# A pad of 32 bytes ahead of the ring of split weights

## The chip, the core and the metric

The kernel runs on one core of one Trainium2 chip. The metric is the device time of one execution in microseconds. One program is built and launched once; all inputs lie in the chip's memory when the clock starts.

## What is computed

One layer of a hybrid decoder trunk on a sequence of 256 tokens of width 4096, in float32. Cut to what matters:

```
h    = rmsnorm(x, ln_g)                       # 256 x 4096
proj = h @ w_in                               # 4096 x 12288: pool, attention, state space and their gates
y_pool = pool_mixer(p_x, w_pool, pool_scale)
y_attn = stick_breaking_attention(q, k, v)    # 16 heads of 128
y_ssm  = s5_mixer(s_u, ...)                   # scan over the tokens, GELU, then a GLU: h @ w_glu (1024 x 2048)
y      = concat(rmsnorm(branch) * silu(gate)) # 256 x 4096
x      = x + y @ w_out                        # 4096 x 4096
out    = rmsnorm(x, final_g)
```

The three products with w_in, w_glu and w_out are nearly all of the arithmetic. The result has to be of float32 quality.

## The kernel before, in words

**Precision by splitting.** Every big product is made of three fp32r matmuls (one pass of TensorE each, with operands rounded by the engine). Each operand is split into a rounded part, hi, and the rest, lo; the product is x_hi w_hi + x_hi w_lo + x_lo w_hi. ScalarE makes hi by a copy that rounds (line 126), VectorE makes lo as the difference (line 236).

**Which operand is which.** The activations are stationary: the tile `xhl` holds 32 slices of 128 rows, each as hi and lo for 256 tokens (128 partitions x 64 KiB). The weights are moving: they arrive in pieces of 128 x 1024 floats (tile `w`, four buffers), are split into a pair of tiles `hi` and `lo` of 4 KiB per partition each, and stream through TensorE in runs of 512 columns (2 KiB per partition) into a PSUM bank. So every matmul in the main loops loads 128 x 128 floats as the stationary operand and moves 128 x 512. Line 376 is x_hi w_hi, line 383 is x_hi w_lo, line 384 is x_lo w_hi:

```
o = ps[t][:, at:at + wide]
made = T.matmul(o, stat[:, slot, 0, sl], hi[:, n], start=begin, stop=False, skip_group_check=True)
T.matmul(o, stat[:, slot, 0, sl], lo[:, n], start=False, stop=False, skip_group_check=True)
made = T.matmul(o, stat[:, slot, 1, sl], hi[:, n], start=False, stop=end, skip_group_check=True)
```

**The ring.** The pairs are kept in a ring of four (`RING`), in the pool named `stream`, and splitting runs two pieces ahead of the products (`SPLIT_AHEAD`). In the output projection two more pairs are added from another pool (tiles `hix`, `lox`).

**Stages.** First come 24 units of 16 pieces for w_in, four units of 4 pieces for w_glu (whose stationary operand is the tile `hhl`), then four units of 32 pieces for w_out. Between the units' matmuls the program places the side work: the scan's small matmuls (line 714, 742), transposes against an identity (lines 434 and 846), pooling (515, 516, 523), attention (775 to 806). In the output projection a part of the pieces goes through `mm_seven` (line 315), which makes seven products where the plain form makes eight, with sums of rows `y` as stationary operand in some of them. Side work for VectorE and ScalarE is handed out by counters per piece; SyncE issues nearly all loads. The order on each engine is made by the scheduler when the program is built.

**Where tiles lie.** A partition's memory is a stack from the left and one from the right. Every tile takes a multiple of 32 bytes. From the left come the constants and small sums (pool `const`), then `xhl`, then the ring, then everything that opens later on the left (masks, u, attention's tiles, `hhl`, the rows `y`, the two added pairs). The loads `w`, the working tiles of 4 KiB and the scan's tiles lie on the right. The pools are opened in this order:

```
cp = pool("const")
xp = pool("xhl")
wp = pool("stream")
bp = pool("base", side="right")
fp = pool("loads", side="right")
```

In the built program `xhl` begins at byte 5792 of each partition, the four `hi` at 71328, 75424, 79520 and 83616, the four `lo` at 87712, 91808, 95904 and 100000. All of these are 32 above a multiple of 64. The same holds for the other tiles that the fp32r matmuls read (`hhl`, `y`, the added pairs, attention's `tneg`, `ah`, `ax`), for the pooling's and attention's operands and for the mask in bf16; of the matmuls' operands only the identity (byte 4224) is at a multiple of 64. The runs of 512 columns and the slices of 128 columns are whole multiples of 64 bytes, so each operand begins where its tile does, up to such a multiple.

Of the kernel before, what the change touches and what calls it, by code (L numbers as in the profile page):

```python
# [12 lines left out]
F32 = mybir.dt.float32  # L13
# [7 lines left out]
P = 128  # L21
# [62 lines left out]
def body(tc, a, out, ctx):  # L84
# [13 lines left out]
    def pool(name, bufs=1, **kw):  # L98
        return ctx.enter_context(tc.tile_pool(name=name, bufs=bufs, **kw))

    cp = pool("const")
    xp = pool("xhl")
    wp = pool("stream")
    bp = pool("base", side="right")
    fp = pool("loads", side="right")
# [1154 lines left out]
def build(nc, arrays):  # L1260
    a = {k: nc.dram_tensor("in_" + k, v.shape, mybir.dt.from_np(v.dtype), kind="ExternalInput").ap() for k, v in arrays.items()}
    out = nc.dram_tensor("out", (L, D), F32, kind="ExternalOutput").ap()
    with tile.TileContext(nc, schedule_with_timeline_sim=True) as tc:
        with ExitStack() as ctx:
            body(tc, a, out, ctx)
# [8 lines left out]
```

## Time and profile before

| what | value |
|---|---|
| median of 2 runs | 1505.53 us (1505.07 to 1505.99) |
| the profiled execution's own time | 1505.46 us |
| its span, first to last instruction | 1503.7 us |
| mean granted TensorE clock | 0.997 |
| TensorE matmul busy | 1491.0 us, 6850 matmuls |
| weight load busy | 1231.9 us |
| VectorE busy | 1224.2 us |
| ScalarE busy | 883.6 us |
| data moved | 424.50 MB, mean 282 GB/s |

How to read it: PE is TensorE's matmuls, PEld its loads of the stationary operand, which run beside the matmuls. A matmul's duration in the profile is longer than the distance to the next one's start, since matmuls are pipelined: in the main loops a matmul of 0.39 us starts every 0.23 us. A busy share of 99% therefore says that TensorE is never out of work, not how fast it works. The distance between the starts, called the pitch here, is what adds up to the span.

### The profile page before, as it was taken

The page shows a single profiled execution, that of the slowest core. Times are in us where ns is not written, and L with a number is a line of the kernel's source. Part 1 is how long each engine was busy: PE and PEld are TensorE (multiplying, and loading weights), DVE is VectorE, ACT ScalarE, POOL GpSimd, SP SyncE. Part 2 cuts the span into 40 slices and gives each one's busy share as a digit, 9 for nine tenths or more (in the row PEclk, how much of TensorE's full clock was granted, in tenths as well). Part 3 has the DMA queues.
Part 4 walks back from the last instruction along what each step waited for, and adds up shares of the span by engine and source line. Part 5 has one row for each costly group of instructions (what it writes and reads, how often), then busy time and mean ns, then how long its engine had stood idle before and what let it go on. Part 6 is the DMA issues. An engine that isn't in the chain of part 4 may idle for free.

```text
span 1503.7 us, 19837 instructions
## 1 busy us (share of the span) xinstructions
PE 1491.0 (99%) x6850; PEld 1231.9 (82%) x6850; DVE 1224.2 (81%) x1876; ACT 883.6 (59%) x1166; POOL 15.2 (1%) x31
## 2 busy tenths in 40 slices
PE   9999999999999999999999999999999999999996
PEld 7888888888888888888888888888888888888885
DVE  7479978898999898998975555686657998989887
ACT  7655456665655555555655544665546776757574
POOL 0000000000000000000000000000000000000000
PEclk9999999999999999999999999999999999999998
DMA  9866556676788887888788788798977998989795
GB/s 357 308 226 207 194 172 212 197 229 232 267 301 306 295 302 249 307 298 300 239 293 284 272 299 282 268 338 314 339 246 249 367 369 324 333 307 353 271 365 222
DMA packets 129364, 424.50 MB, mean 282 GB/s; under 512 B 15472, under 2 KB 21360, under 8 KB 129264
## 3 DMA queue, kind: packets, MB, share of 16 engines
q1 hardware_dynamic: 115504, 398.17, 75.3%
q10 hardware_dynamic: 10000, 10.92, 2.5%
q0 software_dynamic: 3760, 14.16, 2.5%
q8 instruction: 53, 0.87, 0.2%
q14 instruction: 47, 0.39, 0.1%
HBM read 371.28 MB, written 48.76 MB: 279 GB/s over the span
## 4 chain that ended last, share of the span: by engine, by line
PE 99%; DVE 1%; ACT 0%; issue 0%; DVEq 0%
PE pm L376 27%; PE pm L383 27%; PE pm L384 27%; PE p L315 8%; PE pm L315 6%; PE ps_c L846 1%; PE ps_bu L714 1%; PE ps_y L742 1%; PE ps_t L434 0%; PE ps_z L775 0%; PE ps_p L523 0%; PE ps_i L151 0%; PE ps_z L793 0%; PE ps_av L805 0%; PE ps_av L806 0%; PE ps_av L804 0%
## 5 line engine op out<-in xcount | busy, mean ns | idle before, releaser
L236 DVE TENSOR_TENSOR lo<-w,hi 128x1024 fp32r<-128x1024 f32 (+1 forms) x531 | 619.0, 1172 | 226.2 <-ACT hi L126 224.2
L126 ACT ACTIVATE hi<-w 128x1024 fp32r<-128x1024 f32 (+1 forms) x531 | 537.7, 1019 | 441.0 <-PE pm L384 357.9
L383 PE MATMUL pm<-lo,xhl 128*128 128x512 f32 x1710 | 667.1, 390 | 0.0
L384 PE MATMUL pm<-hi,xhl 128*128 128x512 f32 x1710 | 666.8, 390 | 0.0
L376 PE MATMUL pm<-hi,xhl 128*128 128x512 f32 x1710 | 658.2, 391 | 0.0
L376 PEld LDWEIGHTS pm<-hi,xhl 128*128 128x128 f32 x1710 | 321.2, 188 | 66.0 <-ACT hi L126 0.6
L383 PEld LDWEIGHTS pm<-lo,xhl 128*128 128x128 f32 x1710 | 321.2, 188 | 65.8 <-DVE lo L236 0.7
L384 PEld LDWEIGHTS pm<-hi,xhl 128*128 128x128 f32 x1710 | 321.2, 188 | 65.5
L236 DVE TENSOR_TENSOR lo<-t,hi 128x1024 fp32r<-128x1024 f32 x84 | 100.5, 1219 | 10.7 <-ACT hi L126 10.0
L126 ACT ACTIVATE hi<-t 128x1024 fp32r<-128x1024 f32 x84 | 87.3, 1055 | 34.0 <-PE pm L384 11.6
L315 PE MATMUL pm<-hi,xhl 128*128 128x512 f32 x168 | 65.3, 390 | 0.0
L315 PE MATMUL p<-hi,xhl 128*128 128x512 f32 x168 | 65.2, 389 | 0.0
L315 PE MATMUL p<-hi,y 128*128 128x512 f32 x168 | 64.5, 389 | 0.0
L126 ACT ACTIVATE tr<-et,pw 128x32 f32<-128x32 f32 (+3 forms) x128 | 45.2, 385 | 22.4 <-DVE et L123 9.1
L123 DVE SCALAR_TENSOR_TENSOR et<-et,pw,tr 128x16 f32<-128x16 f32 (+3 forms) x256 | 55.7, 274 | 2.9 <-ACT tr L126 2.7
L114 DVE TENSOR_TENSOR pre<-pre 128x512 f32<-128x512 f32 (+2 forms) x72 | 49.6, 689 | 1.0
L729 DVE TENSOR_TENSOR_SCAN tb<-rho,ta 128x256 f32<-128x256 f32 x64 | 40.5, 674 | 0.2
L315 PEld LDWEIGHTS p<-hi,xhl 128*128 128x128 f32 x168 | 31.5, 188 | 6.5
L315 PEld LDWEIGHTS p<-hi,y 128*128 128x128 f32 x168 | 31.5, 188 | 6.5
L315 PEld LDWEIGHTS pm<-hi,xhl 128*128 128x128 f32 x168 | 31.5, 188 | 6.5
L315 PE MATMUL p<-lo,y 128*128 128x512 f32 x84 | 32.7, 389 | 0.0
L315 PE MATMUL p<-lo,xhl 128*128 128x512 f32 x84 | 32.7, 389 | 0.0
(278 smaller groups left out, 1171.9 us busy)
## 6 DMA issues: line engine op xcount, KB each, us to landing
w<-in_ws SPq DMA_DIRECT2D x492, 512.0 KB, 5.0
pre<-in_ws SPq DMA_DIRECT2D x68, 512.0 KB, 7.1
sums<-pre SPq DMA_DIRECT2D x68, 512.0 KB, 5.6
t<-sums SPq DMA_DIRECT2D x68, 512.0 KB, 7.3
w<-in_ws SPq DMA_DIRECT2D x38, 256.0 KB, 7.0
xsq<-in_xr SPq DMA_DIRECT2D x8, 512.0 KB, 6.7
o<-in_xr SPq DMA_DIRECT2D x8, 512.0 KB, 7.7
xt<-in_xT SPq DMA_DIRECT2D x15, 256.0 KB, 6.1
```

Source lines behind the costliest of these rows:

```text
L114: V.tensor_tensor(o, x, y, op)
L123: V.scalar_tensor_tensor(o, x, s, y, op0, op1)
L126: return S.activation(o, x, f, **kw)
L236: low = V.tensor_tensor(dst_lo, src, dst_hi.bitcast(F32), ALU.subtract)
L315: T.matmul(o, stat[:, p, :], pair[q][:, n], start=start and k == 0, stop=stop and k == 2, skip_group_check=True)
L376: made = T.matmul(o, stat[:, slot, 0, sl], hi[:, n], start=begin, stop=False, skip_group_check=True)
L383: T.matmul(o, stat[:, slot, 0, sl], lo[:, n], start=False, stop=False, skip_group_check=True)
L384: made = T.matmul(o, stat[:, slot, 1, sl], hi[:, n], start=False, stop=end, skip_group_check=True)
L714: T.matmul(ps[:, c, :], b3r[:, j, c, :], u3r[:, j, :], start=c == 0, stop=True, skip_group_check=True)
L729: V.tensor_tensor_scan(tb[:, c, :], rho[:, pr:pr + 1].broadcast_to([P, L]), ta[:, c, :], 0.0, ALU.mult, ALU.add)
L742: made = T.matmul(ps[32 * j:32 * j + 32, 0:L], cf[:, j, c, :], ss[j][:, c, :], start=c == 1, stop=c == 0, skip_group_check=True)
L846: T.transpose(ps[:, (c * 2 + t) * P:(c * 2 + t + 1) * P], z[:, t, (h * 2 + c) * P:(h * 2 + c + 1) * P], ident)
```

## The change

A pool of its own with one tile of 32 bytes per partition is opened between `xhl` and the ring. Nothing writes or reads the tile.

```
 
     cp = pool("const")
     xp = pool("xhl")
+    pool("even").tile([P, 8], F32, name="even")
     wp = pool("stream")
     bp = pool("base", side="right")
     fp = pool("loads", side="right")
```

In the built program `xhl` stays at 5792; the `hi` begin at 71360, 75456, 79552 and 83648, the `lo` at 87744, 91840, 95936 and 100032, which are multiples of 64. All that stands behind them on the left moves by 32 as well, and so also begins at multiples of 64: the moving operands of the main loops and of attention's fp32r matmuls, and with them `hhl` and the rows `y`, the stationary operands of the GLU and of a part of the output projection. The tiles on the right stay where they were. The instructions, their order on every engine and their waits are the same as before.

More of the change, by code (lines that the diff above doesn't have):

```diff
@@ L102, in body @@
     xp = pool("xhl")
+    pool("even").tile([P, 8], F32, name="even")
     wp = pool("stream")
```

## The prediction

> **What bounds the kernel now.** I read the profile page first: the totals of the engines, the granted clock, and the shares of the chain that ended last.
>
> ```profile
> span 1503.7 us, 19837 instructions
> PE 1491.0 (99%) x6850; PEld 1231.9 (82%) x6850; DVE 1224.2 (81%) x1876; ACT 883.6 (59%) x1166; POOL 15.2 (1%) x31
> PEclk9999999999999999999999999999999999999998
> DMA  9866556676788887888788788798977998989795
> PE 99%; DVE 1%; ACT 0%; issue 0%; DVEq 0%
> L126 ACT ACTIVATE hi<-w 128x1024 fp32r<-128x1024 f32 (+1 forms) x531 | 537.7, 1019 | 441.0 <-PE pm L384 357.9
> ```
>
> TensorE is the chain from end to end, at the full granted clock, and does not wait for its operands: it is ScalarE that stands idle, 357.9 us of it until line 384's matmul gives a ring buffer back. The time is thus a count of matmuls times their pitch. Four views, each limited to one line over the whole span, count those of the main loops (lines 376, 383, 384 and 315 in this order; the number behind the x):
>
> ```profile
> 0.00:1503.70 1503.70, 684.06 (x1778) 334.01 (x1778) 1.00 0.81 282
> 0.00:1503.70 1503.70, 693.19 (x1778) 334.02 (x1778) 1.00 0.81 282
> 0.00:1503.70 1503.70, 693.03 (x1778) 333.94 (x1778) 1.00 0.81 282
> 0.00:1503.70 1503.70, 201.35 (x882) 165.39 (x882) 1.00 0.81 282
> ```
>
> That is 6216, of which the last 12 are 256 columns wide: 6204 matmuls of 512 columns. Their pitch I take from the timeline of the last stage, whose first column is the start:
>
> ```profile
> 1480.64 0.39 PE L383 MATMUL pm<-lo,xhl 128*128 128x512 f32 x1
> ...
> 1490.38 0.39 PE L384 MATMUL pm<-hi,xhl 128*128 128x512 f32 x1
> 1490.61 0.28 PE L376 MATMUL p<-hi,xhl 128*128 128x256 f32 x1
> 1490.72 0.28 PE L383 MATMUL p<-lo,xhl 128*128 128x256 f32 x1
> ...
> 1491.92 0.28 PE L384 MATMUL p<-hi,xhl 128*128 128x256 f32 x1
> ```
>
> From 1480.64 to 1490.61 are 44 steps in 9.97 us: 226.6 ns each. 6204 x 226.6 ns is 1405.8 us of the 1503.7. With 256 columns the first step is 0.11 us and the following ten are 1.20 us, 120 ns each: a stationary operand can be loaded that often at least, so its load does not set the 226.6.
>
> **Is 226.6 ns the array's own pace?** Other matmuls of the same program say no. The groups with shapes kept apart (number behind the bar: busy us, mean ns), and the timeline at one pooling step:
>
> ```profile
> L384 PE MATMUL pm<-hi,xhl 128*128 128x512 f32 x1710 | 666.8, 390 | 0.0
> L523 PE MATMUL ps_p<-wpl,pT 128*128 128x256 f32 x32 | 7.5, 378 | 0.0
> L515 PE MATMUL ps_p<-band,px 128*128 128x256 f32 x16 | 4.8, 379 | 0.0
> L794 PE MATMUL ps_z<-ah,oneneg 128*128 128x256 f32 x8 | 2.2, 278 | 0.0
> L778 PE MATMUL ps_z<-maskb,identb 128*128 128x256 bf16 x8 | 2.2, 273 | 0.0
> 151.97 1.89 PE L523 MATMUL ps_p<-wpl,pT 128*128 128x256 f32 x8
> 153.50 0.58 PE L383 MATMUL pm<-lo,xhl 128*128 128x512 f32 x1
> ```
>
> Line 523 multiplies plain float32, and takes eight records for four matmuls of 256 columns. Eight of them last 1.89 us together, the last one 0.378, so seven steps are 1.51 us: 215.7 ns. That is 256 columns in the time that a bf16 matmul of 256 columns would use twice (273 ns long where this is 378), so a plain float32 column takes two of the array's column times, 512 in all. An fp32r matmul of 512 columns also has 512 column times, one per column, yet is 390 ns long, not 378, and has a pitch 10.9 ns longer. With 256 columns the excess is half: 278 against 273 for the bf16 form. So the excess grows with the columns: 10.9 ns over 2048 bytes of each partition, 0.34 ns per 64 bytes, a little under one column time (215.7 / 512 = 0.42 ns). And what differs is the rate of reading: 4 bytes per column time and partition in fp32r, 4 per two in plain float32, 2 per one in bf16. These slower readers begin at 32 above a multiple of 64 too and show no excess.
>
> This is the picture on which I forecast: at the full reading rate, a stream that begins half-way in a 64-byte piece straddles a boundary in each piece and loses about a column time there; slower streams have the room to hide it. The trace has no fp32r matmul whose moving operand begins at a multiple of 64, so it cannot show this; that the loss per 64 bytes comes out near one column is what speaks for it.
>
> In the Trainium skill, "TensorE: Matmul & The Clock Gate", section "Back-to-back issue gap", the warm gap is given as N / 2.4 + 2.5 ns, 215.8 for 512 columns. The plain float32 rows agree (215.7), the fp32r rows differ by 10.8; were the rule to hold for fp32r once aligned, the sum would be 67 us less, the same as by the rows.
>
> **The change part by part.** No instruction, order or wait changes. The pad's tile is never written: no cost.
>
> *The moving operands.* If the excess goes, 6204 x 10.9 ns = 67.6 us leave the chain. The bounds: nothing goes (0), or the new pitch is shorter than line 523's by what the rows' hundredths leave open, 0.01 us over seven steps, 1.4 ns or 9 us more (76.5). I take 67.6, since line 523 is the nearest row.
>
> *The stationary operands.* `xhl` stays. The loads take 188 ns (334 us over 1778) and fit in 215.7; whether `hhl` and `y` load faster does not matter.
>
> *Splitting.* ScalarE writes `hi`, VectorE reads it and writes `lo`, now at other addresses. No row shows these at a multiple of 64. If VectorE's split lengthened by the same sixteenth, 531 operations of 1172 ns (row below) would take 39 us more of VectorE, spread over a span in which it has 280 us idle; if it shortened, nothing on the chain moves. I take zero on the chain and keep 5 us for the tight places.
>
> *What is late next.* At the new pitch a stretch of 50 us becomes 47.6. These are the tightest (columns: PE, PEld, VectorE, ScalarE, POOL, clock, DMA share, GB/s):
>
> ```profile
> L236 DVE TENSOR_TENSOR lo<-w,hi 128x1024 fp32r<-128x1024 f32 (+1 forms) x531 | 619.0, 1172 | 226.2 <-ACT hi L126 224.2
> 300.00:350.00 50.00, 50.00 (x228) 41.50 (x228) 48.92 (x80) 29.86 (x40) 1.07 (x2) 1.00 0.69 222
> 450.00:500.00 50.00, 50.00 (x228) 41.49 (x227) 48.21 (x86) 25.30 (x34) 0.00 (x0) 1.00 0.92 321
> 1150.00:1200.00 50.00, 50.00 (x226) 41.40 (x225) 48.68 (x83) 37.72 (x48) 0.00 (x0) 1.00 0.90 331
> 1200.00:1250.00 50.00, 50.00 (x222) 41.42 (x221) 45.67 (x54) 35.20 (x41) 0.00 (x0) 1.00 0.99 378
> ```
>
> VectorE has 48.92, 48.21 and 48.68 us of work there, 1.3, 0.6 and 1.1 more than fits; the DMA engines, busy 0.99 of 50 us, have 1.9 too much. That is 4.9 us given back. Shorter stretches inside the others must also hit a full VectorE, so my estimate is 8 us, between 4.9 and 15. The last 12 us behind the last matmul (1491.92 to 1503.7) do not change.
>
> *The sum.* Against the profiled execution's own 1505.46 us, 0.07 under the median, so nothing is to be corrected: 1505.5 - 67.6 + 8 = 1445.9, say 1446 us.
>
> **The rivals.**
>
> *Nothing changes.* The excess may belong to reading 4 bytes per column time as such, a rate that the memory misses by a sixteenth wherever the stream begins. For it: the pitch is the same for `hi` and `lo`, every buffer and every stage, as a fixed rate would be; against it: nothing in this trace, since all fp32r operands begin alike. The pad then does to the time nothing: 1505 us, give or take 3. In the Trainium skill, "SBUF — State Buffer", section "Specifications (TRN2)", the memory's line is 16 bytes; by that, both places are line starts and this rival holds. No run here shows such a line. The same outcome follows if the granule were 128 bytes: the ring then begins at 64 above a multiple (71360), as far off as before.
>
> *Only the beginning costs.* 2048 bytes from the middle of a 64-byte piece touch 33 pieces, aligned ones 32. One piece is 16 columns, 16 x 0.42 = 6.7 ns; the rest of the excess stays. 6204 x 6.7 = 41.6 us less, some 3 given back: 1467 us. Against it is the excess that halves with 256 columns.
>
> *Slower: the two read streams fall out of step.* After each break the fp32r matmuls run slower for some steps and then fall into the steady pitch:
>
> ```profile
> 9.94 0.40 PE L384 MATMUL pm<-hi,xhl 128*128 128x512 f32 x1
> 10.18 0.39 PE L376 MATMUL pm<-hi,xhl 128*128 128x512 f32 x1
> 10.41 0.39 PE L383 MATMUL pm<-lo,xhl 128*128 128x512 f32 x1
> 10.63 0.39 PE L384 MATMUL pm<-hi,xhl 128*128 128x512 f32 x1
> 10.86 0.39 PE L376 MATMUL pm<-hi,xhl 128*128 128x512 f32 x1
> ```
>
> From 9.94 to 10.41 the steps are 235 ns, behind it 225. If the steady state needs moving and stationary operand at the same place within 64 bytes, the pad takes that away wherever `xhl` is the stationary operand, and at most all 6204 matmuls run as after a break: 6204 x 8.4 = 52 us more, 1558 us. It decides from a pitch of 231.5 on (30 us over 6204). Against it: `hi`, `lo` and `xhl` already differ by every multiple of 64 and all settle.
>
> **How the numbers follow.** The forecast gets 0.50, the partial gain 0.07, no change 0.35, slower 0.08. The nearness to one column per 64 bytes, and slower readers without the excess, put the forecast ahead; that no row shows an aligned stream keeps the second large. A measurement of this kernel tells about 2% (30 us) from no change, so: faster 0.57, within 2% 0.35, slower 0.08. The forecast's own range is 1430 (nothing given back, 1505.5 - 67.6 = 1438, and the 9 us of the bound) to 1460 (15 given back and 5 for the splits, 1458). To leave out no more than 2 in 10 the range must reach the unchanged time: 1430 to 1508.
>
> **What would show it.** Right: rows of lines 376, 383 and 384 at 378 ns instead of 390, a pitch near 215.7 in the last stage, line 794 at 273, plain float32 and bf16 rows unchanged, VectorE's busy time as before at a share of 85%, and some new idle time of PEld released by line 126 or 236 between 300 and 750 us and near 1200. A pitch of 226.6 in the last stage makes the forecast wrong at its first step; a pitch of 220 speaks for the beginning alone; a pitch of 215.7 there with a span above 1460 means that splitting or loading took over.

## The result, and the profile after

The changed kernel takes **1540.74 us** (median of two runs, 1540.67 to 1540.81) where the kernel before takes 1505.53. The ratio is 1.0236, with a 95% interval from 1.0219 to 1.0252. That is slower by 35.2 us. The forecast was 1446 us, its range ended at 1508, and slower had a chance of 0.08: the prediction was wrong in its sign.

The profiled execution took 1540.81 us at the same granted clock (0.997). These are the span, the totals of the engines and the chain that ended last, from its page:

```profile
span 1539.0 us, 19837 instructions
PE 1526.5 (99%) x6850; PEld 1230.2 (80%) x6850; DVE 1228.6 (80%) x1876; ACT 884.9 (58%) x1166; POOL 15.2 (1%) x31
PE 99%; DVE 1%; ACT 0%; issue 0%; DVEq 0%
```

The number of instructions is the same, TensorE is still the whole chain, and its busy time rose by 35.5 us, as much as the span (35.3). So TensorE does not wait: the matmuls themselves have become longer. The costliest groups of the page say which (behind the bar: busy us, mean ns of one):

```profile
L237 DVE TENSOR_TENSOR lo<-w,hi 128x1024 fp32r<-128x1024 f32 (+1 forms) x531 | 620.0, 1174 | 249.6 <-ACT hi L127 247.6
L384 PE MATMUL pm<-lo,xhl 128*128 128x512 f32 x1710 | 676.6, 396 | 0.0
L385 PE MATMUL pm<-hi,xhl 128*128 128x512 f32 x1710 | 676.2, 396 | 0.0
L377 PE MATMUL pm<-hi,xhl 128*128 128x512 f32 x1710 | 667.1, 396 | 0.0
L384 PEld LDWEIGHTS pm<-lo,xhl 128*128 128x128 f32 x1710 | 320.6, 188 | 76.5 <-DVE lo L237 0.9
```

Line numbers are one higher than before. A matmul with `xhl` as the stationary operand lasts 396 ns where it lasted 390; its load still lasts 188. The matmuls whose stationary operand (`hhl` or `y`) lies behind the pad, and so moved along with the ring, stand among the groups with shapes kept apart:

```profile
L384 PE MATMUL pm<-lo,hhl 128*128 128x512 f32 x64 | 24.9, 390 | 0.0
L316 PE MATMUL p<-lo,y 128*128 128x512 f32 x84 | 32.7, 390 | 0.0
L316 PE MATMUL p<-hi,y 128*128 128x512 f32 x168 | 65.4, 394 | 0.0
```

In the kernel before, the last of them was:

```profile
L315 PE MATMUL p<-hi,y 128*128 128x512 f32 x168 | 64.5, 389 | 0.0
```

The GLU's matmuls have not changed, though their moving operands begin at multiples of 64 now like all the others. Of those with `y`, the ones with `lo` have hardly changed (390 where it was 389), but the ones with `hi` have (394 where it was 389). In the order of `mm_seven` it is the ones with `hi` that stand next to matmuls with `xhl`: about half of them have a load of `xhl` beside them. The pitch shows the same for `xhl` and `hhl`. Here is the timeline of three stages, an early one (`xhl` stationary), the GLU (`hhl` stationary) and the last one (`xhl` again); the first column is the start:

```profile
59.66 0.39 PE L377 MATMUL pm<-hi,xhl 128*128 128x512 f32 x1
...
61.76 0.63 PE L377 MATMUL pm<-hi,xhl 128*128 128x512 f32 x2
...
999.67 0.39 PE L384 MATMUL pm<-lo,hhl 128*128 128x512 f32 x1
...
1002.16 0.39 PE L377 MATMUL pm<-hi,hhl 128*128 128x512 f32 x1
...
1524.24 0.40 PE L384 MATMUL pm<-lo,xhl 128*128 128x512 f32 x1
...
1526.11 0.28 PE L377 MATMUL p<-hi,xhl 128*128 128x256 f32 x1
1526.22 0.28 PE L384 MATMUL p<-lo,xhl 128*128 128x256 f32 x1
...
1527.39 0.28 PE L385 MATMUL p<-hi,xhl 128*128 128x256 f32 x1
```

Nine steps in 2.10 us are 233.3 ns, the last stage's eight in 1.87 us are 233.8, and the GLU's eleven in 2.49 us are 226.4, as before. `xhl` is the stationary operand in 5634 of the 6204 matmuls with 512 columns. At 233.3 instead of 226.7 they would take 37.2 us more; 35.2 was measured, 6.2 ns for each. Both traces hold the same 6850 matmuls in the same order, so the steps can be compared one by one. With `xhl`, 5183 steps that were at the steady pitch went from 226.7 to 233.3, which makes 34.3 us. The other 451, most of them longer already and near side work, have not grown. The matmuls with `y` add 1.4 us.

### The profile page after: what moved, and what is told of

Its sections match the earlier page's. It is cut to its first block, busy times and chain, and to the rows that moved or that the text cites. A ratio compares the mean times of both kernels' runs of the same rounds, so it can differ in the third digit from the quotient of the medians.

```text
span 1539.0 us, 19837 instructions
## 1 busy us (share of the span) xinstructions
PE 1526.5 (99%) x6850; PEld 1230.2 (80%) x6850; DVE 1228.6 (80%) x1876; ACT 884.9 (58%) x1166; POOL 15.2 (1%) x31
## 4 chain that ended last, share of the span: by engine, by line
PE 99%; DVE 1%; ACT 0%; issue 0%; DVEq 0%
PE pm L384 27%; PE pm L377 27%; PE pm L385 27%; PE p L316 8%; PE pm L316 6%; PE ps_c L847 1%; PE ps_bu L715 1%; PE ps_y L743 1%; PE ps_t L435 0%; PE ps_z L776 0%; PE ps_p L524 0%; PE ps_i L152 0%; PE ps_z L794 0%; PE ps_av L806 0%; PE ps_av L807 0%; PE ps_av L805 0%
## 5 line engine op out<-in xcount | busy, mean ns | idle before, releaser
L237 DVE TENSOR_TENSOR lo<-w,hi 128x1024 fp32r<-128x1024 f32 (+1 forms) x531 | 620.0, 1174 | 249.6 <-ACT hi L127 247.6
L384 PE MATMUL pm<-lo,xhl 128*128 128x512 f32 x1710 | 676.6, 396 | 0.0
L385 PE MATMUL pm<-hi,xhl 128*128 128x512 f32 x1710 | 676.2, 396 | 0.0
L377 PE MATMUL pm<-hi,xhl 128*128 128x512 f32 x1710 | 667.1, 396 | 0.0
L316 PE MATMUL pm<-hi,xhl 128*128 128x512 f32 x168 | 66.3, 395 | 0.0
L316 PE MATMUL pm<-lo,xhl 128*128 128x512 f32 x84 | 33.2, 395 | 0.0
```

The lines of the kernel that those rows point to most:

```text
L237: low = V.tensor_tensor(dst_lo, src, dst_hi.bitcast(F32), ALU.subtract)
L316: T.matmul(o, stat[:, p, :], pair[q][:, n], start=start and k == 0, stop=stop and k == 2, skip_group_check=True)
```

## The experiments

**Theory and rivals.** The pad changes two things: the place of the moving operand in the memory, and its distance from `xhl`. The theory after the result was that the distance counts: fp32r matmuls of 512 columns run at 226.7 ns when the stationary and the moving operand begin at the same place within some unit, and slower otherwise. The first rival was the prediction's own picture with its sign turned: the absolute place counts, and a multiple of 64 is the bad one. The second was a contest by amount, in which the load takes reading time from the stream wherever the two lie. The expectations call the theory A, the first rival B and the prediction's own picture C. Where they speak of A64 and A256, these are the theory with a unit of 64 or 256 bytes.

The full kernels below change nothing but pads. The small programs leave the whole model out: they run rows of matmuls from two tiles, `stat` and `mov`, with the loads and runs of the main loops.

### Both operands moved

```diff
     cp = pool("const")
+    pool("even").tile([P, 8], F32, name="even")
     xp = pool("xhl")
     wp = pool("stream")
```

> The pad of 32 bytes stands ahead of the activations, so stationary and moving operands both begin at multiples of 64 (and 64 above a multiple of 128). Theory A (the pitch depends on whether the two operands begin at the same place within 64 bytes): pitch 226.7 ns, 1505 us. Theory B (a moving operand at a multiple of 64 is slow, one at 32 is fast, whatever the stationary one does): pitch 233, 1540 us. Theory C of the prediction (a read from the middle of a 64-byte piece costs extra, and only the stationary operand is still there in the changed kernel): pitch 215.7, about 1446 us.

Measured: 1505.98 us against 1505.32, ratio 1.0005 (0.9996 to 1.0014). `xhl` begins at 5824 and the ring at 71360, both multiples of 64, with the old distance of 65536 between them. The row of line 385 is back at its old duration:

```profile
L385 PE MATMUL pm<-hi,xhl 128*128 128x512 f32 x1710 | 666.9, 390 | 0.0
```

The ring lies exactly where the changed kernel has it, and 35 us are gone. So its own place is not the cause. It is also the forecast's test in a pure form, with all operands of the main loops at multiples of 64, and it gains nothing.

### Only the stationary operand moved

```diff
     cp = pool("const")
+    pool("even").tile([P, 8], F32, name="even")
     xp = pool("xhl")
+    pool("even2").tile([P, 8], F32, name="even2")
     wp = pool("stream")
```

> Pads of 32 bytes ahead of and behind the activations: the stationary operand begins at a multiple of 64, the moving one at 32 above it, the reverse of the change. Theory A: the two differ, pitch 233, about 1540 us. Theory B: the moving operand is at 32, pitch 226.7, 1505 us. Theory C: something between 1446 and 1505 us.

Measured: 1540.98 us, ratio 1.0240 (1.0223 to 1.0257). Now `xhl` (5824) is at a multiple of 64 and the ring (71392) is 32 above one, the reverse of the changed kernel, at the same distance, and the time is the same. Together with the changed kernel and the one before this settles that the distance between the operands, not the place of either, makes the 35 us.

### A pad of 64 bytes

```diff
     xp = pool("xhl")
+    pool("even").tile([P, 16], F32, name="even")
     wp = pool("stream")
```

> The pad is 64 bytes in place of 32: both operands begin 32 above a multiple of 64 as before, but at different places within 128 bytes. Theory A (granule of 64 bytes): 226.7 ns and 1505 us. If the granule in which the two have to agree is 128 bytes: slower, 1520 to 1545 us.

Measured: 1518.36 us, ratio 1.0087 (1.0072 to 1.0102): 13.0 us more than before, 2.3 ns in each of 5634 matmuls, a pitch of 229.0. The row of line 385 stands between the two others:

```profile
L385 PE MATMUL pm<-hi,xhl 128*128 128x512 f32 x1710 | 671.5, 393 | 0.0
```

So a unit of 64 bytes is wrong: 64 bytes apart is neither as good as 0 nor as bad as 32.

### The pitch by itself

The program runs sixteen rows of 180 matmuls; each row adds an offset, in floats, to the stationary tile (`so`) and the moving tile (`mo`), and in the last four rows fewer columns are loaded.

```
T.matmul(ps[0:cols, :], stat[:, so + 128 * j:so + 128 * j + cols], mov[:, mo + 512 * m:mo + 512 * m + 512], ...)
```

> Leaves the whole model out: a program of sixteen batches of 180 fp32r matmuls of 512 columns with constant data in the order of the main loops (one stationary slice twice, then the next), each batch with its own offsets. Letters a, b, c, d, e, f, g, h stand for offsets of 0, 32, 16, 48, 8, 4, 64 and 128 bytes; stat or mov says which operand is shifted, both says that both are. half and quart have stationary slices of 64 and 32 columns. Theory A: both_a, both_b, both_c, stat_g and stat_h at 226.7 ns, stat_b and mov_b at 231 to 236, the offsets of 4 to 16 bytes somewhere between or worse. Theory B: mov_b alone is fast. If the 226.7 ns itself holds a cost of loading the stationary operand beside the stream (32 column times for its 128 columns), half_a falls to about 220 and quart_a to 217; if it belongs to the stream alone, both stay at 226.7.

The timeline shows each row as one entry: start, length, and behind the x the count. The pitch is the distance to the next start over 180.

```profile
60.69 40.99 PE L43 MATMUL both_b<-mov,stat 128*128 128x512 f32 x180
101.52 42.16 PE L43 MATMUL stat_b<-mov,stat 128*128 128x512 f32 x180
143.52 42.16 PE L43 MATMUL mov_b<-mov,stat 128*128 128x512 f32 x180
185.51 42.16 PE L43 MATMUL stat_c<-mov,stat 128*128 128x512 f32 x180
...
519.97 41.58 PE L43 MATMUL half_a<-mov,stat 128*64 128x512 f32 x180
561.38 41.86 PE L43 MATMUL half_b<-mov,stat 128*64 128x512 f32 x180
603.07 41.86 PE L43 MATMUL quart_a<-mov,stat 128*32 128x512 f32 x180
644.77 43.31 PE L43 MATMUL quart_b<-mov,stat 128*32 128x512 f32 x180
```

Both moved by 32 bytes: 226.8 ns. Either one alone moved by 32 bytes: 233.3, with the rest of the model gone. So the model's numbers, 226.7 and 233.3, are the two operands' own doing. Three expectations were missed: moved by 64 and by 128 bytes, `stat` gives 233.3 and 232.4 and not 226.7, and both moved by 16 bytes give 231.1. The rows with 64 and 32 columns loaded speak against the contest by amount, and were expected at 220 and 217 if it held: with a half and a quarter of the load, and no offset, the pitch is 230.1 and 231.7, longer than with the whole. With 32 bytes between, half of the load gives 231.7, and a quarter 239.8 (its 43.31 us less the last matmul's own 0.39, over 179 steps).

### The unit, and what bf16 does

Sixteen rows of 120 with `stat` moved by 0, 32, ... 480 bytes (st_a to st_p), two of bf16, and four in which the same two operands are used again and again; behind them single matmuls, each after a row of twelve.

```
for n in range(16):
    batch("st_" + "abcdefghijklmnop"[n], 8 * n, 0)
batch("bf_a", 0, 0, bstat, bmov)
batch("bf_b", 16, 0, bstat, bmov)
```

> Leaves the whole model out: batches of 120 fp32r matmuls of 512 columns in the order of the main loops. st_a to st_p shift the stationary operand by 0, 32, 64 ... 480 bytes against the moving one. Theory A, widened after the first probe (the two must begin at the same place within a longer period, 512 bytes, which is the length of one stationary slice): st_a at 226.7 ns, all fifteen others at 228 to 236. Rival: some other distance is as good or better (a value near 215.7 would be a way to a faster kernel). bf_a and bf_b are the same in bf16 with 0 and 32 bytes: 215.7 both, if only the rate of 4 bytes per column time is touched. fix_a, fix_b, fix_c, fix_d use one stationary and one moving slice throughout, with the stationary one 0, 512, 1024 and 256 bytes off: 226.7 for the first three if 512 is the period, about 232 for the last. iso_a, iso_b, iso_c are single fp32r matmuls with moving operands at 0, 32 and 64 bytes whose stationary load is held back until the matmuls before are over, and iso_p one in plain float32 with the same 512 column times: if the excess over plain float32 is a contest between stream and load, iso_a to iso_c are as long as iso_p (379 ns); if it belongs to the stream, they are 389 or more.

From the timeline (120 matmuls to the entry):

```profile
161.58 28.15 PE L53 MATMUL st_f<-mov,stat 128*128 128x512 f32 x120
189.57 27.63 PE L53 MATMUL st_g<-mov,stat 128*128 128x512 f32 x120
217.03 28.16 PE L53 MATMUL st_h<-mov,stat 128*128 128x512 f32 x120
245.03 27.37 PE L53 MATMUL st_i<-mov,stat 128*128 128x512 f32 x120
272.24 28.15 PE L53 MATMUL st_j<-mov,stat 128*128 128x512 f32 x120
...
467.68 26.07 PE L53 MATMUL bf_a<-bmov,bstat 128*128 128x512 bf16 x120
493.59 26.06 PE L53 MATMUL bf_b<-bmov,bstat 128*128 128x512 bf16 x120
```

160 bytes give 233.3 ns, 192 give 228.8, 224 give 233.3, 256 give 226.8 and 288 again 233.3. The first row, at 0, begins with slower steps (its 120 take 249.3 ns on average) and settles at 226.7. With that, all sixteen in order and within 0.1: 226.7, 233.3, 233.3, 234.2, 232.4, 233.3, 228.9, 233.3, and then the same eight again. The unit is 256 bytes. The models agree: the ring 32 bytes higher is the stationary operand 224 bytes ahead within 256 (st_h, 233.3), the ring 64 bytes higher is 192 (st_g, 228.9, where the full kernel has 229.0). The direction counts: 64 bytes the other way is 233.3. In bf16 the pitch is 215.9 (467.68 to 493.59), and the row with 32 bytes between is as long (26.06 us after 26.07): at this distance, the only one tried, bf16 does not show the effect. The expectation for the fourth row of repeated operands (256 bytes apart), some 232, was missed: it stands at 226.7 like the three others, as the unit of 256 says. The single matmuls last 388 ns with the moving operand at 0 and 397 with it at 32 and at 64 bytes, one in plain float32 mostly 377 to 379. A later experiment takes them up.

### Pads of 160 and 256 bytes

```diff
     xp = pool("xhl")
+    pool("even").tile([P, 40], F32, name="even")
     wp = pool("stream")
```

> The pad between activations and ring is 160 bytes, so the stationary operand stands 96 bytes behind the moving one within 256. Theory A256 (what counts is the distance of the two operands modulo 256 bytes, with the pitches of the second probe): 234.3 ns in the 5634 matmuls whose stationary operand is xhl, 5634 x 7.67 = 43 us more, about 1548 us. Theory A64 (only same or not the same place within 64 bytes): as the change, 1541 us.

Measured: 1545.67 us, ratio 1.0268 (1.0250 to 1.0285). 40.3 us over 5634 matmuls are 7.2 ns, a pitch of 233.8; the small program's row at 96 bytes (st_d), which is this distance, has 234.2. The time lies between the two forecasts, 2 us below the one and 5 above the other. It is clearly slower than the pad of 32 bytes, which a unit of 64 can't give.

For 256 bytes the tile has `[P, 64]`:

> The pad is 256 bytes. Theory A256: distance 0 modulo 256, pitch 226.7, 1505 us. If the distance must be 0 modulo 512 or the kernel's own slot distances matter beyond the probe: slower, 1518 us or more.

Measured: 1505.15 us against 1505.34, ratio 0.9998 (0.9989 to 1.0008). A pad eight times as large as the change's costs nothing. These two, forecast from the small program, confirm the unit of 256 bytes in the full kernel.

### Fewer columns, and places that alternate

Rows of 120 with 512, 448, 384 and 320 columns, once at the same place (ln) and once 32 bytes apart (lm); then pairs in which each second matmul has its stationary (alts) or its moving operand (altm) 32 bytes on.

```
for name, so, cols in (("ln_a", 0, 512), ("ln_b", 0, 448), ("ln_c", 0, 384), ("ln_d", 0, 320),
                       ("lm_a", 8, 512), ("lm_b", 8, 448), ("lm_c", 8, 384), ("lm_d", 8, 320)):
```

> Leaves the whole model out. ln_a to ln_d: 512, 448, 384 and 320 columns with both operands at the same place; lm_a to lm_d the same with the stationary operand 32 bytes off. If the excess grows with the columns (one column time in 16): 226.7, 198.3, 170.0, 141.7 for ln, and 233.3, 204, 175, 146 for lm. If it is a fixed sum per matmul (32 and 48 column times): 226.7, 200.0, 173.3, 146.7 and 233.3, 206.7, 180, 153.3. alts: the stationary operand alternates between 0 (alts_a) and 32 bytes (alts_b) under a moving one at 0; altm the moving one alternates. If a matmul's own stationary place decides, alts_a steps are near 226.7 and alts_b steps near 233; if the place of the operand that is loaded beside the stream decides, the reverse. iso, isq, ish: single matmuls of 512, 384 and 256 columns with nothing before or beside them on TensorE; a has the operands at the same place, b and c are 32 bytes off, d is 256 off. If the excess needs a load beside the stream, all iso are 379 long; if it comes from the relation of the two operands alone, iso_a and iso_d are 388 and iso_b and iso_c 397.

```profile
72.00 20.99 PE L51 MATMUL ln_c<-mov,stat 128*128 128x384 f32 x120
92.83 17.76 PE L51 MATMUL ln_d<-mov,stat 128*128 128x320 f32 x120
110.42 28.16 PE L51 MATMUL lm_a<-mov,stat 128*128 128x512 f32 x120
138.42 24.69 PE L51 MATMUL lm_b<-mov,stat 128*128 128x448 f32 x120
162.94 20.98 PE L51 MATMUL lm_c<-mov,stat 128*128 128x384 f32 x120
183.75 17.76 PE L51 MATMUL lm_d<-mov,stat 128*128 128x320 f32 x120
201.35 0.39 PE L58 MATMUL alts_a<-mov,stat 128*128 128x512 f32 x1
```

At the same place 384 columns take 173.6 ns and 320 take 146.6. With 226.7 for 512 the slope from 320 to 512 is 80.1 / 192 = 0.417 ns a column, one column time, and what is left is a fixed sum: 226.7 - 512 x 0.417 = 13 ns for every matmul, with 320 columns too (146.6 - 133.4; the row with 448 is a little off this line, 202.7 - 186.8 = 16). So what fp32r pays beyond its column times does not grow with the columns. At 32 bytes apart, 512 columns take 233.3 and 448 take 204.3, against 226.7 and 202.7; with 384 and 320 the distance no longer matters (173.4 and 146.7, behind 173.6 and 146.6). A fixed price for the distance, expected at 180 and 153.3 there, was missed.

Two parts gave no clear answer. With the stationary operand alternating the mean pitch is 235.0 (240 matmuls in 56.40 us); both theories had half of the steps long, so 230; with the moving operand alternating it is 230.0. Both values fit roughly if a step is long when either its own stationary operand or the one loaded beside it lies off its stream: then every step is long in the first row, every second one in the second. The changed kernel's trace points the same way: where a load of `xhl` runs beside a matmul with `y` the step rose from 226.6 to 232.4, and where a load of `y` runs beside a matmul with `xhl` from 226.5 to 231.7 (129 steps each). No experiment was made to test this reading. And single matmuls with their load held back came out alike at every distance (494 to 503 ns with 512 columns), but their durations, much above 388, may hold the load as well and the granted clock averaged 0.79 there, so that says nothing.

### Every four bytes

72 rows of 60: `stat` moved by 0, 4, ... 252 bytes (d_aa on), then both moved together by 0, 4, ... 28 (d_hb on).

```
so, mo = (n, 0) if n < 64 else (n - 64, n - 64)
```

> Leaves the whole model out: 72 batches of 60 fp32r matmuls of 512 columns. The first 64 (d_aa to d_ha) put the stationary operand 0, 4, 8 ... 252 bytes behind the moving one; the last eight shift both by 0, 4 ... 28 bytes. Theory A256 (the pitch follows the distance of the two operands modulo 256 bytes): 226.7 ns at 0 only, 228.9 at 192, 232.4 at 128, 233.3 at 32, 64, 160 and 224, 234.3 at 96, and in between values of the same size, 228 to 240. Rival: a distance that is no multiple of 32, which no layout of whole tiles reaches, is faster than 226.7; it would make a faster kernel. Both operands shifted alike: 226.7 if only the distance counts, 231 where the first probe saw 16 bytes.

From the timeline, the rows at 120 bytes and at both moved by 4:

```profile
439.59 13.77 PE L51 MATMUL d_dd<-mov,stat 128*128 128x512 f32 x60
453.20 14.06 PE L51 MATMUL d_de<-mov,stat 128*128 128x512 f32 x60
...
926.04 14.42 PE L51 MATMUL d_hc<-mov,stat 128*128 128x512 f32 x60
940.30 14.09 PE L51 MATMUL d_hd<-mov,stat 128*128 128x512 f32 x60
```

At 120 bytes the pitch is 226.8. Once settled, this value is reached at 0, 100, 120, 132, 144, 156, 228 and 252 bytes and undercut at none; the worst is 237.2, at 164. Of the multiples of 32, where tiles can lie, only 0 reaches it. Below 32 bytes the place itself matters as well: both operands moved by 4 give 237.7 at a distance of 0. None of the layouts tried is faster than that of the kernel before, which has the distance between `xhl` and the ring at 0.

### One matmul behind a row

A row of 24 matmuls (`run`, both operands at place 0 in the four "zero" cases and 32 bytes on in the four "moved"), then a single one with a stationary operand of its own and nothing to load beside it. The two offsets of a case are those of the single matmul's stationary and moving operand.

```
for name, run, so, mo in (("zero_a", 0, 0, 0), ("zero_b", 0, 8, 0), ("zero_c", 0, 0, 8), ("zero_d", 0, 8, 8),
                          ("moved_a", 8, 0, 0), ("moved_b", 8, 8, 0), ("moved_c", 8, 0, 8), ("moved_d", 8, 8, 8)):
```

> Leaves the whole model out: single matmuls of 512 columns, 6 of each kind, each behind a row of 24 and with nothing loaded or streamed beside it; only its own stationary load lies beside the last stream of the row. zero: the row has both operands at 0, moved: both at 32 bytes. a: the single one has stationary and moving operand at 0 and 0, b: 32 and 0, c: 0 and 32, d: 32 and 32. Theory own (the stream is slowed by its distance to its own stationary operand): zero_a, zero_d, moved_a, moved_d are 388 ns long, the other four 397. Theory before (what counts is the distance to the stream ahead of it): zero_a, zero_b, moved_c, moved_d 388, the others 397. Theory beside (contest of the stream with a load at the same time): all eight alike, near 379.

The groups with shapes kept apart give the single one's duration, mean of six:

```profile
L62 PE MATMUL zero_a<-mov,fresh 128*128 128x512 f32 x6 | 2.3, 388 | 0.0
L62 PE MATMUL zero_c<-mov,fresh 128*128 128x512 f32 x6 | 2.4, 397 | 0.0
L62 PE MATMUL moved_a<-mov,fresh 128*128 128x512 f32 x6 | 2.3, 388 | 0.0
L62 PE MATMUL moved_b<-mov,fresh 128*128 128x512 f32 x6 | 2.4, 397 | 0.0
```

That all are alike, because nothing is loaded beside them, is refuted: 388 and 397. That the distance to the row's stream decides holds in six of eight: zero_a, zero_b (389) and moved_d (388) at the row's place, zero_c, zero_d and moved_b (397) away from it. It fails for moved_a, which is away from the row and 388, and moved_c has 392. That its own two operands decide holds in five of eight; zero_d, with both at the same place, has 397. So what decides a matmul with no load beside it stays open. The profile's ends of matmuls are modelled, too, which makes durations weaker evidence than starts.

The row's last matmul gives a clean answer, from starts alone. Beside it, the single one's stationary operand is loaded. The timeline, in windows around the end of a row, shows the row's last two and the single one behind them (zero_d, then moved_b):

```profile
155.73 0.62 PE L58 MATMUL run<-mov,stat 128*128 128x512 f32 x2
156.19 0.40 PE L62 MATMUL zero_d<-mov,fresh 128*128 128x512 f32 x1
...
249.62 0.61 PE L58 MATMUL run<-mov,stat 128*128 128x512 f32 x2
250.07 0.40 PE L62 MATMUL moved_b<-mov,fresh 128*128 128x512 f32 x1
```

Two pitches are 0.46 us when the load lies 32 bytes off the stream and 0.45 when it lies at its place. Summed over the six pairs of a case they are 2.76 to 2.78 us in the four cases with the load 32 bytes off (zero_b, zero_d, moved_a, moved_c) and 2.70 to 2.73 in the four at the same place; the means, 2.770 and 2.718, differ by 9 ns a pair. So a load lengthens the stream that runs beside it when the two lie at different places; in these eight cases the single one's own distance plays no part in it. The 9 ns are near the 6.6 ns by which the pitch rose in the changed kernel, and not the same: how the one becomes the other in a steady row is not shown.

## Why the prediction was wrong

*What bounds the kernel* was right. The time is a count of matmuls times their pitch, nothing waits, and the longer pitch of the 5634 matmuls with `xhl`, some 6 ns each, is nearly the whole of the 35.2 us.

*"So the excess grows with the columns"* is the step that failed, and all of the 67.6 us hung on it. It compared durations: 390 against 378 with 512 columns, 278 against 273 with 256. The row with 278 was one of several. The same view of the kernel before has these for fp32r matmuls of 256 columns:

```profile
L795 PE MATMUL ps_z<-ax,tneg 128*128 128x256 f32 x8 | 2.3, 281 | 0.0
L383 PE MATMUL p<-lo,xhl 128*128 128x256 f32 x4 | 1.1, 283 | 0.0
```

Against 273 they are 8 and 10 ns longer, not 5: nearer to the 12 with 512 columns than to half of it. The trace of before also had a better measure, the pitch, and the prediction printed it: 226.6 with 512 columns and 120 with 256. Their difference is 106.6 ns for 256 columns, one column time each, and 13 ns remain in both cases. The prediction used the 120 to show that the load does not set the pitch, and did not ask what it says of the excess. The rows with 320 and 384 columns show the fixed sum directly. An excess that is the same for 1280 and for 2048 bytes is no loss per 64 bytes, so the picture of straddled pieces had nothing left to stand on; with all operands of the main loops at multiples of 64 the kernel took 1505.98 us. Since the excess does not grow with the bytes, a loss per 64 bytes has no meaning, and that it came near one column time was a coincidence.

The Trainium skill, "TensorE: Matmul & The Clock Gate", section "Back-to-back issue gap", gives N / 2.4 + 2.5 ns as the warm gap of an isolated matmul, from which 215.8 for 512 columns is an estimate. The bf16 rows agree (215.9); fp32r does not come below 226.7 at any of the 64 distances. The same page of the Trainium skill, section "Step-by-step: what each phase is for", says that a load takes no reading bandwidth from the running matmul, since the two have ports of their own. The measurement differs, and decides: in the last experiment a load at another place cost the fp32r matmul beside it some 9 ns.

*The stationary operands* got one sentence, that `xhl` stays and its loads fit. This is the other half of the mistake, a term put at nothing: by staying, `xhl` lost its place relative to the ring, and that made the 35 us. The loads do fit (188 ns before and after), and what changed is the pitch of the stream beside them.

*Splitting costs nothing on the chain* was right: VectorE's split took 1174 ns where it took 1172, with the `hi` and `lo` at other addresses. (The "same sixteenth" that it weighed there does not match its own sum: 10.9 of 215.7 ns is a twentieth.)

*What is late next* was never reached, since no time was gained.

*The rival on the slower side* had the right sign and the nearest mechanism: moving and stationary operand need the same place within a unit. It gave 1558 us and needed a pitch of 231.5; the pitch was 233.3, and the time 1540.74. That the streams fall out of step, as after a break, is not shown. Two things in it were off besides. The price, 8.4 ns for all 6204 matmuls, was some 6 for the 5634 with `xhl`, because `hhl` and `y` moved along. And what stood against it, that `hi`, `lo` and `xhl` already differ by every multiple of 64 and all settle, was false. The ring's first `hi` is 65536 bytes behind `xhl`, a pair's tiles are 4096 long, and slices and runs are 512 and 2048: every distance in the kernel before is a multiple of 512, so also of 256. The addresses in the description of the kernel were enough to see it, and would have told that the trace of the main loops had only ever shown one distance within 256. It was the only thing said against this rival, which got 0.08.

*Nothing changes* had a chance of 0.35. Its idea of the excess, a cost of fp32r as such wherever the stream begins, fits the runs better than the forecast's, as far as that the excess stays at every place. The Trainium skill, "SBUF — State Buffer", section "Specifications (TRN2)", has lines of 16 bytes, as cited with this rival. They do not account for the result: a move by 32 bytes, two such lines, changes the pitch from 226.7 to 233.3. Nor is it a granule of 128 bytes: in the built small programs `mov` begins at byte 53376, a multiple of 128, and the best pitch there is 226.7 as well.

*Only the beginning costs* falls with the forecast: a run of columns that begins at a multiple of 64 saves nothing (1505.98 us with both operands moved).

**What stays open.** The experiments show that with places at multiples of 32 the distance within 256 bytes sets the pitch, and that a load acts on the stream beside it. What has this unit of 256 bytes is not shown. Nor is the nature of the some 13 ns that the fp32r matmuls of 256 to 512 columns pay at the best distance (16 with 448), or why a single matmul with no load beside it takes 388 or 397 ns. For the alternating rows at 235.0 there is a reading that fits, and no test of it.

## What to carry to other kernels

When a loop reads two operands at once, work out their distance as well as their places before moving one of them: a kernel's usual sizes can hold a distance at a good value that no line of it asks for. With fp32r matmuls of 512 columns on this chip, keep stationary and moving tiles a multiple of 256 bytes apart; here a pad of 32 cost 2.4%, one of 256 nothing. And to ask whether a cost is fixed or grows with the size, compare pitches of two sizes, not the durations of pipelined instructions.

## What had not been expected of the hardware

- With a load for each, the pitch of fp32r matmuls with 512 columns depends on the operands' distance with a period of 256 bytes: 226.7 at 0, 228.9 at 192 and 232.4 to 234.2 at the other multiples of 32. bf16 has 215.9 with and without 32 bytes between.
- A smaller load is no help at the same place: 64 and 32 columns loaded give 230.1 and 231.7 where 128 give 226.7.
- The 12 matmuls of 256 columns are a little faster in the changed kernel, not slower: in its last stage ten steps from 1526.22 to 1527.39 us are 117 ns each, against 120 before.
